# Key preparation only behind decay steps, two gate tiles ahead of the last merge, and a later transpose in z

## The chip, the cores and the metric

The kernel runs on one core of a Trainium2 chip. The metric is the device time of one execution in microseconds (us), from the first to the last instruction. The engines are named as in the profile: PE is TensorE's matmuls, PEld its weight loads, DVE VectorE, ACT ScalarE, POOL GpSimd and SP SyncE, whose queue issues the DMAs. Each engine works through its own queue in order and waits on semaphores for the others.

## The reference

Two layers of a hybrid mixer over 512 latent and 256 context tokens, in float32, with 1024 channels. Each layer normalises its input, makes one input projection and runs three branches over it: attention (8 query heads, 2 key heads, normalised queries and keys with rotary positions), a bidirectional state-space scan (SSD) in chunks of 128 tokens, and a gated convolution of 31 taps. The branches are merged by sigmoid gates and projected back. Cut to what matters here:

```python
q, k, v, ga, xbc, dt, z, glu, gcv, gm = split_in(h @ w_in)
qh = apply_axial_rope(rmsnorm(heads_q(q), q_norm_w), rope)
kh = apply_axial_rope(rmsnorm(heads_kv(k), k_norm_w), rope)
ua = merge_heads(latent_attention(qh, kh, heads_kv(v), kh_c, vh_c)) * jax.nn.silu(ga)
us = rmsnorm(y * jax.nn.silu(z), ssd_norm_w)          # y: the scan's output
uc = conformer_conv(glu, gcv, cm_conv_w, cm_conv_b, cm_ln_w, cm_ln_b)
g = jax.nn.sigmoid(gm.reshape(gm.shape[:-1] + (N_BRANCH, D_MODEL)) + b_gate)
y = (g[..., 0, :] * (ua @ w_br_attn) + g[..., 1, :] * (us @ w_br_ssd)
     + g[..., 2, :] * (uc @ w_br_conv))
x_new = x + gate * (y @ w_out)
```

In the last layer context tokens give only keys, values and scan states, so most tiles there have 512 columns in place of 768.

## The kernel before, in words

Every product of a float32 activation with a weight is made of three matmuls: both operands are split into a rounded high part and a remainder (`hh` and `hl`, `whi` and `wlo`). `wload` loads a weight tile (`raw`) and splits it on ScalarE (`whi`, L156) and VectorE (`wlo`, L157). Channel-major products run through `mm_cm_steps` (L175), 24 matmuls for 8 input tiles or 12 for 4, with two accumulator banks (`pj`).

A layer goes through these stages: the convolution branch's projection; keys, values and step sizes (`ps_kvd`); the eight x, B and C tiles (`ps_xbc`); z (`ps_z`); queries (`ps_q`); layer norm of the convolution; the scan with the merge of the convolution branch as filler; attention with the merge of the scan branch as filler; the merge of the attention branch; the output projection (`ps_o`). From the key projection to the end of attention the order of TensorE's instructions is as the code is written; the other engines' order, and TensorE's outside that stretch, is set by a scheduler.

Three things are touched by the change.

*The B tiles.* Tiles 0 to 5 of x and B are transposed (`xbc_turn`, `pt_x`) some tiles after their projection: the loop over `ps_xbc` takes them from the list `late` once it holds two, which leaves the last (tile 5, the second B tile) for the loop over z. The first B tile is transposed in the loop over `ps_xbc`.

*Key preparation.* `qk_prep` makes a key pair (`khl`, into `kk`) or a query pair (`qhl`, into `qt`) of 256 tokens ready in three turns: first squares (`qsq`), their sum (`qrs`, with a power on GpSimd) and the rotation, then the split into high part and remainder, then eight transposes (`pt_qk`), which ScalarE empties bank by bank. `Pipe.turn` moves each pair in work on by one turn and starts the next: three key pairs, then query pairs. The list `main` holds the steps of the scan: `begin`, `decay` (matrices `am` and `al`, matmuls `pseg`, `ew`, `wt`), `inner` (matmuls `pyd` on `wt`), `state` and `end`. After each step `sf.fill` issues some matmuls of the filler (merge `ps_gm` and `ps_br`, attention gates `ps_ga`, gate tiles made ahead). Once the filler's merge is done, every other step is followed by a turn. After the `us` transposes the rest of the turns follow, until three key pairs and one query pair are done:

```python
while pipe.done < NTT // 2 + 1:
    sf.fill(qk_turns / 2)
    pipe.turn()
```

with `qk_turns` 2 in the first layer and 0 in the second. Then attention begins with `ps_l`, the scores, which feed `mx` and the exponentials (`pe`).

*The last merge.* `merge_steps` goes over eight channel tiles. For each it makes the gate (`sig_steps`: 24 matmuls `ps_gm`, then `tg` on ScalarE), or loads it if it was made ahead (`AHEAD_TILES`, the odd ones), multiplies the branch output (`ps_br`) by it, adds the sum so far (`yo`, loaded) and splits the result (`yh`, `yl`). `tg`, `yo` and the loaded attention outputs (`og`) share three buffers (`fill`). Just before, attention ends with `po_v`, `oa` and the split `ua`.

Of the kernel before, what the change touches and what calls it, by code (L numbers as in the profile page):

```python
# [15 lines left out]
P = 128  # L16
DM = 1024
KD = DM // P
# [39 lines left out]
def hybrid_kernel(ctx, tc, xT, cc, consts, rope, mod_params, params, fnw, w_mod, w_cm, w_q, w_kvd, w_z,  # L58
# [18 lines left out]
    def bigt(shape, dt, name):  # L77
        return big.tile(shape, dt, tag="S", name=name)

    def work(shape, dt, name):  # L80
        return wk.tile(shape, dt, tag="W", name=name)

    def small(shape, dt, name):
        return wk.tile(shape, dt, tag="W2", name=name, bufs=7)

    def fill(shape, name):
        return fl.tile(shape, F32, tag="F", name=name)
# [52 lines left out]
    def wload(src, nk, ncol, prio=TOP, keep=None):  # L140

        per, half = {P: (8, 4), 256: (4, 2)}.get(ncol, (2, 2))
        res = []
        with tc.high_priority(offset=prio):
            for k0 in range(0, nk, per):
                n = min(per, nk - k0)
                raw = wp.tile([P, n, ncol], F32, tag="raw", name="raw")
                nc.sync.dma_start(raw, src[:, k0:k0 + n, :])
                for u0 in range(0, n, half):
                    m = min(half, n - u0)  # L150
                    if keep is None:
                        hi = wp.tile([P, m, ncol], F32R, tag="whi", name="whi", bufs=5)
                        lo = wp.tile([P, m, ncol], F32R, tag="wlo", name="wlo", bufs=5)
                    else:
                        hi, lo = (keep[:, i, k0 + u0:k0 + u0 + m, :] for i in range(2))
                    S.activation(hi, raw[:, u0:u0 + m, :], AF.Copy)  # L156
                    V.tensor_tensor(out=lo, in0=raw[:, u0:u0 + m, :], in1=f(hi), op=ALU.subtract)  # L157
                    res += [(hi[:, i, :], lo[:, i, :]) for i in range(m)]
        return res

    def mm_cm_steps(w, xh, xl, ntok, evac, name, col=slice(None), psum=None, late=False, piece=PIECE):

        nk = len(w)
        spans = ntok if isinstance(ntok, tuple) else [(a, min(ntok, a + 512)) for a in range(0, ntok, 512)]
        for a, b in spans:
            ps = (psum or pjt)(name)
            done = 0  # L170
            order = [(k, w[k][i], x) for k in range(nk) for i, x in ((0, xh), (0, xl), (1, xh))]
            if late:
                order.sort(key=lambda o: o[2] is xl)
            for n, (k, st, mv) in enumerate(order):
                T.matmul(ps[:, :b - a], st[:, col], mv(k)[:, a:b], start=(n == 0), stop=(n == len(order) - 1))  # L175
                done += b - a
                if done >= piece and n < len(order) - 1:
                    yield done
                    done = 0
            evac(ps[:, :b - a], a, b)  # L180
            yield done
# [28 lines left out]
    def mm_tm(w, xh, xl, tt, ncol, name):  # L210
        ps = pjt(name)
        nk = len(w)
        t = tok(tt)
        for k in range(nk):
            hi, lo = w[k]
            T.matmul(ps[:, :ncol], xh(k)[:, t], hi, start=(k == 0), stop=False)
            T.matmul(ps[:, :ncol], xh(k)[:, t], lo, start=False, stop=False)
            T.matmul(ps[:, :ncol], xl(k)[:, t], hi, start=False, stop=(k == nk - 1))
        return ps
# [153 lines left out]
    for li in range(2):  # L373
        last = li == 1
        par = sm.tile([P, NPAR], F32, tag="par", name="par")
        nc.sync.dma_start(par, params[li])
        ntok = NL if last else NT
# [73 lines left out]
        def conv(n, after=None):  # L451
            with tc.issue_after(after.ins) if after is not None else nullcontext():
                for _ in range(n):
                    next(taps, None)

        for ct in range(4):
# [10 lines left out]
            tg = fill([P, ntok], "tgl")  # L467
# [72 lines left out]
        late, soon = [], []  # L540
# [42 lines left out]
        for b in range(2):  # L583
            w = wload(w_z[li, b], KD, 256)
            for tt in range(ntt):
                ps = mm_tm(w, xh, xl, tt, 256, "ps_z")
                zs = small([P, 256], F32, "zs")
                S.activation(zs, ps[:, 0:256], AF.Silu)
                for fn in soon:
                    fn()  # L590
                soon = []
                nc.sync.dma_start(z_dr[tt][:, b * 256:(b + 1) * 256], zs)
                if late and tt > 0:
                    late.pop(0)()
                conv(2, xm)

# [86 lines left out]
        def then(fn, steps):  # L683

            done = 0
            for n in steps:
                yield n
                done += n
                if done >= MOD_LAG and fn is not None:
                    fn()  # L690
                    fn = None
            if fn is not None:
                fn()

        def sig_steps(br, ct, tg):
            w = wload(w_cm[li, C_GM + br * 8 + ct], KD, P)
            yield from mm_cm_steps(w, xh, xl, ntok,
                                   lambda ps, a, b: S.activation(tg[:, a:b], ps, AF.Tanh, scale=0.5,  # L698
                                                                 bias=hw[:, br * 8 + ct:br * 8 + ct + 1]), "ps_gm")
# [8 lines left out]
        def merge_steps(br, u, first, fin, ready=()):  # L708
            if fin:
                yh.extend(bigt([P, 4, ntok], F32R, "yh") for _ in range(2))  # L710
                yb = bigt([P, 4, ntok], F32R, "yl")
                yl.extend([yb[:, i, :] for i in range(4)] + [work([P, ntok], F32R, "yl") for _ in range(4)])
            end = None
            next_mods = Mods(1, mods[1], 8 * (2, 1, 0)[br])
            for ct in range(KD):
                if ct % 2 == 0:
                    wb = wload(w_br[li, br, ct // 2], 4, 256)
                if not first:
                    yo = fill([P, ntok], "yo")
                    nc.sync.dma_start(yo, y_dr[ct][:, :ntok])  # L720
                if ct in ready and not last:
                    tg = mid.tile([P, ntok], F32, tag="H", name="tgr", bufs=2)
                else:
                    tg = fill([P, ntok], "tg")
                c0 = (ct % 2) * P

                def br_out(ps, a, b):
                    V.scalar_tensor_tensor(out=tg[:, a:b], in0=tg[:, a:b], scalar=1.0, in1=ps, op0=ALU.add,  # L728
                                           op1=ALU.mult)

                if ct in ready:
                    nc.sync.dma_start(tg, g_dr[ct][:, :ntok])
                else:
                    yield from then(end, sig_steps(br, ct, tg))
                    end = None
                yield from then(end, mm_cm_steps(wb, lambda k: u[0][:, k, :], lambda k: u[1][:, k, :], ntok, br_out,
                                                 "ps_br", slice(c0, c0 + P)))
                end = None
                if not first:
                    V.tensor_tensor(out=tg, in0=tg, in1=yo, op=ALU.add)  # L740
                if not fin:
                    nc.sync.dma_start(y_dr[ct][:, :ntok], tg)
                else:
                    a, b = yh[ct // 4][:, ct % 4, :], yl[ct]
                    S.activation(a, tg, AF.Copy, scale=0.5)
                    V.scalar_tensor_tensor(out=b, in0=tg, scalar=0.5, in1=f(a), op0=ALU.mult, op1=ALU.subtract)
                if not last and ct % 2 == 1:
                    end = next_mods.visit()
                    yield 2048
            if end is not None:  # L750
                end()
# [204 lines left out]
        decays = [partial(ch.decay, g) for ch in chunks for g in range(2)]  # L956
# [28 lines left out]
                   len(main) + end_turns + 4 * us_turns + qk_turns)  # L985
        pipe, kk = Pipe(), None

        since = 0
        for step in main:
            step()  # L990
            sf.fill()
            if merged[0]:
                if kk is None:
                    kk = bigt([P, 2, KVH, NT], F32R, "kk")
                    qts.append(bigt([P, 4, ntok], F32R, "qt"))
                    pipe.todo += [partial(k_prep, t0) for t0 in range(0, NTT, 2)]
                    pipe.todo += [partial(q_prep, 0, t0) for t0 in range(0, ntt, 2)]
                since += 1
                if since % 2 == 1:
                    pipe.turn()  # L1000
        sf.fill(end_turns)

# [1 line left out]
        for ct in range(4):  # L1004
            nw = par[:, O_SNW + ct:O_SNW + ct + 1]
            for t0, t1 in ((0, NLT), (NLT, ntt))[:1 if last else 2]:
# [3 lines left out]
                a, b, n = t0 * P, t1 * P, (t1 - t0) * P  # L1010
# [318 lines left out]
```

## Time and profile before

| what | us |
|---|---|
| times shown, lowest, median, highest | 1477.03, 2856.81, 3255.66 |
| the profiled execution, own time | 1479.32 |
| its span, first to last instruction | 1477.5 |
| PE busy | 1434.7 |
| PEld busy | 1256.6 |
| DVE busy | 1037.4 |
| ACT busy | 712.7 |

The profile is of one execution. Busy times of different engines overlap. The ends of matmuls are modelled, so the starts tell more than the durations. The granted clock is given as a share of TensorE's full 2.4 GHz: 1.00, or 0.50 for 1.2 GHz.

### The profile page before, as it was taken

Reading aid. Unit: us, or ns where it says so; the run is one execution under the profiler, and the core shown is the slowest. Engines: PE = TensorE matmul, PEld = TensorE weight load, DVE = VectorE, ACT = ScalarE, POOL = GpSimd, SP = SyncE. Lnnn points to the kernel's source line nnn. Section 1 sums busy time; section 2 is a strip of 40 time slices with the busy share of each in tenths; the row PEclk is TensorE's granted clock in tenths of the full one; section 3 lists DMA queues with packets and bytes.
Section 4 is the critical chain, followed back from the end, with each engine's and each line's share of the span. In section 5 each row is a group of like instructions: output and inputs, shape, how many; then the busy total and the mean of one; then the engine's idle time right before and its main releaser. Section 6 shows DMA issues by size and latency. Waiting matters only on the chain. (4 is left out here: it accounts for less than half of the span.)

```text
span 1477.5 us, 24830 instructions
## 1 busy us (share of the span) xinstructions
PE 1434.7 (97%) x9660; PEld 1256.6 (85%) x9660; DVE 1037.4 (70%) x1895; ACT 712.7 (48%) x1580; POOL 81.0 (5%) x177
## 2 busy tenths in 40 slices
PE   5999999999998999999999999999999999999996
PEld 5889899988887888888888888989988887888796
DVE  5689998766557766565444478899877788676464
ACT  4423543365444466566322344354464646666341
POOL 0000010100001210000000000001010121000000
PEclk9999999999999999999999999999999999999998
DMA  9222333213334323323654433223423342323451
GB/s 375 76 73 95 103 126 111 77 61 100 101 105 126 132 90 120 101 74 120 201 170 156 162 118 113 69 62 115 141 76 114 97 145 93 100 93 105 146 171 58
DMA packets 79670, 172.57 MB, mean 117 GB/s; under 512 B 7616, under 2 KB 37440, under 8 KB 79552
## 3 DMA queue, kind: packets, MB, share of 16 engines
q1 hardware_dynamic: 79552, 170.98, 35.3%
q8 instruction: 76, 1.25, 0.4%
q14 instruction: 42, 0.34, 0.1%
HBM read 143.43 MB, written 27.53 MB: 116 GB/s over the span
## 5 line engine op out<-in xcount | busy, mean ns | idle before, releaser
L156 ACT ACTIVATE whi<-raw 128x512 fp32r<-128x512 f32 (+1 forms) x316 | 198.9, 632 | 269.3 <-DMA raw<-in_w_cm_dram 57.1
L157 DVE TENSOR_TENSOR wlo<-raw,whi 128x512 fp32r<-128x512 f32 (+1 forms) x316 | 217.2, 692 | 149.0 <-ACT whi L156 138.2
L445 DVE SCALAR_TENSOR_TENSOR vacc<-vt,par,vacc 128x783 f32<-128x783 f32 (+1 forms) x232 | 206.3, 889 | 8.9 <-ACT vacc L442 5.4
L175 PE MATMUL ps_gm<-hh,whi 128*128 128x512 f32 (+1 forms) x576 | 210.4, 365 | 0.0
L175 PE MATMUL ps_gm<-hh,wlo 128*128 128x512 f32 (+1 forms) x576 | 207.5, 360 | 0.0
L175 PE MATMUL ps_gm<-hl,whi 128*128 128x512 f32 (+1 forms) x576 | 207.4, 360 | 0.0
L175 PEld LDWEIGHTS ps_gm<-hh,whi 128*128 128x128 f32 x576 | 109.1, 189 | 16.5 <-issue 1.5
L175 PEld LDWEIGHTS ps_gm<-hh,wlo 128*128 128x128 f32 x576 | 108.9, 189 | 16.1 <-issue 0.7
L175 PEld LDWEIGHTS ps_gm<-hl,whi 128*128 128x128 f32 x576 | 108.9, 189 | 15.0 <-issue 0.5
L175 PE MATMUL ps_xbc<-hh,whi 128*128 128x512 f32 (+1 forms) x240 | 83.5, 348 | 0.0
L175 PE MATMUL ps_xbc<-hl,whi 128*128 128x512 f32 (+1 forms) x240 | 82.4, 343 | 0.0
L175 PE MATMUL ps_xbc<-hh,wlo 128*128 128x512 f32 (+1 forms) x240 | 82.3, 343 | 0.0
L698 ACT ACTIVATE tg<-ps_gm,hw 128x512 f32<-128x512 f32 x72 | 44.5, 617 | 46.3 <-PE ps_gm L175 45.2
L175 PE MATMUL ps_o<-yh,whi 128*128 128x256 f32 (+1 forms) x208 | 65.8, 317 | 0.5 <-DVE xnew L1158 0.3
L175 PE MATMUL ps_o<-yh,wlo 128*128 128x256 f32 (+1 forms) x208 | 65.8, 316 | 0.0
L175 PE MATMUL ps_o<-yl,whi 128*128 128x256 f32 (+1 forms) x208 | 65.7, 316 | 0.0
L1078 ACT ACTIVATE pth<-pt_p 128x512 f32<-128x512 f32 x72 | 43.3, 604 | 46.0 <-PE pt_p L1072 45.3
L567 DVE SCALAR_TENSOR_TENSOR xacc<-xraw,par,xacc 128x770 f32<-128x770 f32 (+1 forms) x64 | 63.2, 997 | 1.9 <-ACT xacc L564 1.6
L728 DVE SCALAR_TENSOR_TENSOR tg<-tg,ps_br 128x512 f32<-128x512 f32 x66 | 39.6, 600 | 32.6 <-PE ps_br L175 28.8
L1034 DVE TENSOR_REDUCE mx<-ps_l 128x1 f32<-128x512 f32 x64 | 43.5, 688 | 22.7 <-PE ps_l L1028 22.3
L175 PE MATMUL ps_br<-us,whi 128*128 128x512 f32 (+1 forms) x192 | 57.0, 364 | 0.0
L175 PE MATMUL ps_br<-ua,whi 128*128 128x512 f32 (+1 forms) x192 | 54.3, 368 | 2.6 <-ACT ua L1142 2.2
(281 smaller groups left out, 3619.0 us busy)
## 6 DMA issues: line engine op xcount, KB each, us to landing
raw<-in_w_cm_dram SPq DMA_DIRECT2D x96, 512.0 KB, 3.5
raw<-in_w_mod_dram SPq DMA_DIRECT2D x32, 512.0 KB, 5.3
raw<-in_w_br_dram SPq DMA_DIRECT2D x24, 512.0 KB, 3.7
raw<-in_w_out_dram SPq DMA_DIRECT2D x21, 512.0 KB, 3.7
wm<-in_w_mod_dram SPq DMA_DIRECT2D x16, 512.0 KB, 8.9
ydr<-tg SPq DMA_DIRECT2D x16, 384.0 KB, 3.2
yo<-ydr SPq DMA_DIRECT2D x16, 384.0 KB, 3.3
raw<-in_w_z_dram SPq DMA_DIRECT2D x8, 512.0 KB, 3.7
```

Source lines behind the costliest of these rows:

```text
L156: S.activation(hi, raw[:, u0:u0 + m, :], AF.Copy)
L157: V.tensor_tensor(out=lo, in0=raw[:, u0:u0 + m, :], in1=f(hi), op=ALU.subtract)
L175: T.matmul(ps[:, :b - a], st[:, col], mv(k)[:, a:b], start=(n == 0), stop=(n == len(order) - 1))
L445: V.scalar_tensor_tensor(out=acc[:, :n] if j else vt[:, o:o + n], in0=vt[:, o + j:o + j + n], scalar=cw(j), in1=acc[:, :n], op0=ALU.mult, ...
L567: xm = V.scalar_tensor_tensor(out=acc[:, :n], in0=raw[:, j:j + n], scalar=par[:, O_SCW + ct * 5 + j:O_SCW + ct * 5 + j + 1], in1=acc[:, :n ...
L698: lambda ps, a, b: S.activation(tg[:, a:b], ps, AF.Tanh, scale=0.5, bias=hw[:, br * 8 + ct:br * 8 + ct + 1]), "ps_gm")
L728: V.scalar_tensor_tensor(out=tg[:, a:b], in0=tg[:, a:b], scalar=1.0, in1=ps, op0=ALU.add, op1=ALU.mult)
L1034: V.tensor_reduce(out=mx[:, 0, j:j + 1], in_=pl[j], axis=AX.X, op=ALU.max, negate=True)
L1078: S.activation(pf, pt, AF.Copy)
```

## The change

A turn of the key preparation follows only a decay step in place of every other step. In the last merge of the second layer two gate tiles that were not made ahead (channel tiles 0 and 2) are made before the first `ps_br`, and their later place in the loop is skipped. The last B tile's transposes move from the second token tile of z's first half to the first token tile of its second half.

```diff
-                if late and tt > 0:
+                if late and b == 1:
                     late.pop(0)()
...
+            early = {}
+            if fin and last:
+                for ct in [ct for ct in range(KD) if ct not in ready][:2]:
+                    early[ct] = fill([P, ntok], "tg")
+                    yield from sig_steps(br, ct, early[ct])
+            done = set(early)
             for ct in range(KD):
...
-                if ct in ready and not last:
+                if ct in early:
+                    tg = early.pop(ct)
+                elif ct in ready and not last:
                     tg = mid.tile([P, ntok], F32, tag="H", name="tgr", bufs=2)
...
                 if ct in ready:
                     nc.sync.dma_start(tg, g_dr[ct][:, :ntok])
-                else:
+                elif ct not in done:
                     yield from then(end, sig_steps(br, ct, tg))
                     end = None
...
-        since = 0
         for step in main:
             step()
             sf.fill()
...
-                since += 1
-                if since % 2 == 1:
+                if step in decays:
                     pipe.turn()
```

What it does to the queues shows at three places.

ScalarE in the first layer, at the last decay step of the scan; before:

```order
L817 ACTIVATE wt<-gm_4506,dts 128x128 x4
L861 ACTIVATE qsq<-ks 128x256
L665 ACTIVATE ga<-ps_ga 128x512
L156 ACTIVATE whi<-raw 128x512
L889 ACTIVATE khl<-ks 128x2x64 x4
L805 ACTIVATE am<-cst,dah 128x128 x4
L156 ACTIVATE whi<-raw 128x512
L805 ACTIVATE am<-cst,dah 128x128
L665 ACTIVATE ga<-ps_ga 128x256
L805 ACTIVATE am<-cst,dah 128x128 x3
```

And with the change:

```order
L825 ACTIVATE wt<-gm_4506,dts 128x128 x4
L813 ACTIVATE am<-cst,dah 128x128 x8
L869 ACTIVATE qsq<-ks 128x256
L665 ACTIVATE ga<-ps_ga 128x512
L156 ACTIVATE whi<-raw 128x512 x2
L665 ACTIVATE ga<-ps_ga 128x256
L821 ACTIVATE ew<-pseg 128x512
L825 ACTIVATE wt<-gm_4506,dts 128x128 x4
L897 ACTIVATE khl<-ks 128x2x64 x8
```

The eight `am` of the last decay step now stand directly behind `wt`, ahead of the keys' `qsq` and `khl`; both key pairs' `khl` stand behind the next `wt`.

TensorE and ScalarE in the second layer, ahead of the first scores; TensorE before:

```order
L1009 MATMUL pt_us<-mr,xt 128x128 x4
L175 MATMUL ps_gm<-hh,whi 128x512
L175 MATMUL ps_gm<-hl,whi 128x512
L175 MATMUL ps_gm<-hh,wlo 128x512
L175 MATMUL ps_gm<-hh,whi 128x512
L175 MATMUL ps_gm<-hl,whi 128x512
L175 MATMUL ps_gm<-hh,wlo 128x512
L903 MATMUL pt_qk<-mr,khl 128x128 x16
L903 MATMUL pt_qk<-mr,qhl 128x128 x8
L1028 MATMUL ps_l<-kk,qt 128x512 x2
```

TensorE with the change:

```order
L175 MATMUL ps_gm<-hh,whi 128x512
L175 MATMUL ps_gm<-hl,whi 128x512
L175 MATMUL ps_gm<-hh,wlo 128x512
L911 MATMUL pt_qk<-mr,khl 128x128 x24
L911 MATMUL pt_qk<-mr,qhl 128x128 x8
L1034 MATMUL ps_l<-kk,qt 128x512 x2
```

ScalarE there, before:

```order
L861 ACTIVATE qsq<-qs 128x512
L1011 ACTIVATE us<-pt_us,par 128x512
L156 ACTIVATE whi<-raw 128x512
L698 ACTIVATE tg<-ps_gm,hw 128x512
L904 ACTIVATE kk<-pt_qk 128x4x128 x4
L904 ACTIVATE qt<-pt_qk 128x4x128 x2
L896 ACTIVATE qhl<-qs 128x4x64 x2
L1050 ACTIVATE pe,sr<-ps_l,mx 128x512
```

And with the change:

```order
L897 ACTIVATE khl<-ks 128x2x64 x8
L1017 ACTIVATE us<-pt_us,par 128x512
L156 ACTIVATE whi<-raw 128x512
L698 ACTIVATE tg<-ps_gm,hw 128x512
L912 ACTIVATE kk<-pt_qk 128x4x128 x2
L869 ACTIVATE qsq<-qs 128x512
L912 ACTIVATE kk<-pt_qk 128x4x128 x4
L904 ACTIVATE qhl<-qs 128x4x64 x2
L912 ACTIVATE qt<-pt_qk 128x4x128
```

All three key pairs and the first query pair are now transposed in one row. The `qsq` that stood in this stretch was the second query pair's; now it is the first's, which has yet to be rotated, split and transposed before `ps_l`. In the first layer the same stretch has 24 transposes in a row, where it had eight.

ScalarE at the end of attention in the second layer, where the gate tiles `tg` meet the split `ua`; before:

```order
L698 ACTIVATE tg<-ps_gm,hw 128x512
L156 ACTIVATE whi<-raw 128x512
L1142 ACTIVATE ua<-oa 128x512
L1142 ACTIVATE ua<-og 128x512 x2
L698 ACTIVATE tg<-ps_gm,hw 128x512
L1142 ACTIVATE ua<-og 128x512
L156 ACTIVATE whi<-raw 128x512 x2
L745 ACTIVATE yh<-tg 128x512
```

And with the change:

```order
L156 ACTIVATE whi<-raw 128x512
L698 ACTIVATE tg<-ps_gm,hw 128x512
L1148 ACTIVATE ua<-oa 128x512
L1148 ACTIVATE ua<-og 128x512 x2
L698 ACTIVATE tg<-ps_gm,hw 128x512
L156 ACTIVATE whi<-raw 128x512
L1148 ACTIVATE ua<-og 128x512
L156 ACTIVATE whi<-raw 128x512
L698 ACTIVATE tg<-ps_gm,hw 128x512
```

A third `tg` comes ahead of the first `yh`. On TensorE 28 `ps_gm` matmuls follow the last `po_v` where six did, and 48 `ps_br` in a row follow them where 24 did.

## Rows read from the trace of the kernel before

**Rows 1.** The page, part 1: busy us, share of the span, instructions.
```profile
PE 1434.7 (97%) x9660; PEld 1256.6 (85%) x9660; DVE 1037.4 (70%) x1895; ACT 712.7 (48%) x1580; POOL 81.0 (5%) x177
```

**Rows 2.** Waits of PE, whole span: total us, times, longest us.
```profile
PE pseg L810 <- ACT am L805: 3.7, 3, 2.0
...
PE ps_br L175 <- ACT ua L1142: 2.2, 1, 2.2
```

**Rows 3.** Windows: length, busy us (instructions) by engine, granted clock, DMA share, GB/s.
```profile
463.00:466.40 3.40, 1.30 (x4) 0.78 (x5) 3.40 (x13) 3.09 (x10) 0.00 (x0) 1.00 0.60 178
466.40:469.90 3.50, 3.50 (x10) 2.71 (x9) 2.74 (x10) 2.16 (x7) 1.21 (x2) 0.51 0.65 184
...
1224.20:1227.60 3.40, 3.40 (x11) 2.63 (x10) 2.55 (x5) 0.72 (x2) 0.00 (x0) 0.50 0.00 0
...
1377.80:1381.20 3.40, 3.40 (x9) 2.48 (x8) 0.69 (x1) 1.44 (x3) 0.00 (x0) 0.50 0.45 147
```

**Rows 4.** Timeline, first layer, last decay step: start us, us, instruction, idle before.
```profile
463.88 0.50 PE L810 MATMUL pseg<-am,mr 128*128 128x512 f32 x1 [2.04 <-ACT am L805]
...
465.83 0.50 PE L810 MATMUL pseg<-am,mr 128*128 128x512 f32 x1 [1.22 <-ACT am L805]
...
468.56 0.43 DVE L867 TENSOR_TENSOR ks<-ks,qrs 128x256 f32<-128x256 f32 x1 [0.39 <-POOL qrs L138]
...
470.17 0.68 DVE L820 TENSOR_TENSOR wt<-wt,ew 128x512 f32<-128x512 f32 x1
...
470.75 1.00 PE L831 MATMUL pyd<-xt,wt 128*128 128x64 f32 x8
...
472.12 1.39 DVE L769 TENSOR_TENSOR xd<-xt,dd 128x512 f32<-128x512 f32 x1
```

**Rows 5.** Timeline, second layer, round the first scores.
```profile
1201.70 0.80 PE L903 MATMUL pt_qk<-mr,khl 128*128 128x128 f32 x8
...
1202.33 1.96 PE L846 MATMUL po<-st,bc 128*128 128x256 f32 x8
...
1218.31 0.63 ACT L861 ACTIVATE qsq<-qs 128x512 f32<-128x512 f32 x1 [0.89 <-DMA qs<-qdr]
...
1218.97 0.69 DVE L865 TENSOR_REDUCE qrs<-qsq 128x8 f32<-128x512 f32 x1 [0.77 <-ACT qsq L861]
...
1219.76 1.14 PE L903 MATMUL pt_qk<-mr,khl 128*128 128x128 f32 x12
...
1220.88 2.05 ACT L904 ACTIVATE kk<-pt_qk 128x512 fp32r<-128x512 f32 x4
...
1222.02 1.02 PE L903 MATMUL pt_qk<-mr,qhl 128*128 128x128 f32 x8
...
1223.47 0.73 PE L1028 MATMUL ps_l<-kk,qt 128*128 128x512 f32 x2 [0.44 <-ACT qt L904]
...
1225.31 0.75 DVE L897 TENSOR_TENSOR qhl<-qs,qhl 128x256 fp32r<-128x256 f32 x2
```

**Rows 6.** Timeline, second layer, end of attention.
```profile
1373.54 0.67 ACT L698 ACTIVATE tg<-ps_gm,hw 128x512 f32<-128x512 f32 x1
...
1375.82 0.49 PE L175 MATMUL ps_br<-ua,whi 128*128 128x512 f32 x1 [2.15 <-ACT ua L1142]
1376.71 0.50 PE L175 MATMUL ps_br<-ua,whi 128*128 128x512 f32 x1 [0.40 <-DVE ua L1143]
```

**Rows 7.** The chain that ended last: start us, us, what.
```profile
1383.94 5.51 PE ps_gm L175 x24
1389.45 5.61 PE ps_br L175 x24
```

**Rows 8.** DMA issues from 1360 us on: KB each, median us to landing.
```profile
tg<-gdr SPq DMA_DIRECT2D x4, 256.0 KB, 2.6
```

**Rows 9.** Timeline, second layer, the two B tiles' transposes.
```profile
998.87 1.54 PE L537 MATMUL pt_x<-mr,bc 128*128 128x128 f32 x6 [2.40 <-ACT bc L573]
...
1012.43 0.82 PE L537 MATMUL pt_x<-mr,bc 128*128 128x128 f32 x6
```

## The prediction

> **What bounds the kernel now.** I read the page first, then the waits of TensorE, then the granted clock in windows round the waits, and last the timelines at the places that the change touches. The page has TensorE's matmuls busy for 97% of the span [rows 1]. The waits view gives the other side: behind the first weights, the waits that the change can reach are 3.7 us in three for the decay matrices (`pseg` on ScalarE's `am`) and 2.2 us for the attention output (`ps_br` on `ua`) [rows 2]. So VectorE and ScalarE set the time only where TensorE stands still, and an edit is worth what it takes from such a wait or adds to one. A wait has a second price: after three of them the granted clock is 0.51 or 0.50, the lower level, 1.2 GHz, for about 3.4 us, and ahead of the first of them TensorE had worked 1.30 us of 3.4 [rows 3]. At half clock 3.4 us do the work of 1.7, so such a stretch costs up to 1.7 us where TensorE is what the rest waits for.
>
> The sum is made against the profiled execution, 1479.32 us (span 1477.5 and 1.8 around it). That is the scale of the lowest shown time, 1477.03. The median, 2856.81, is nearly twice that; nothing in this trace accounts for it, so I forecast an execution like the profiled one.
>
> **Key preparation, layer 0, at the decay steps.** Before, ScalarE's order has `khl` between `wt` and `am`; `khl` needs VectorE's rotation of the keys, `am` stands behind it, and `pseg` starts at 463.88 after 2.04 us of waiting, then waits 1.2 us more [rows 2, 4]. The order of the changed kernel has all eight `am` ahead of `qsq` and `khl`, so these 3.3 us go. But what is late next? `pyd` needs `wt` times `ew`, which VectorE starts at 470.17 and ends at 470.85; `pyd` starts at 470.75 [rows 4]. VectorE is busy 3.40 us of 3.40 in 463.0 to 466.4 [rows 3]: it is the bound of this place. Ahead of that product its new order leaves out the third key tile's reduction, two multiplications (0.43 us for the one shown) and a `khl` pair (about as long), some 1.7 us as an estimate (four of 0.4), and puts in `xd`, which took 1.39 us before [rows 4]. So `pyd` comes 0.3 to 1.5 us earlier, not 3.3. TensorE then stands in front of `pyd` instead of `pseg`, over 3 us as an estimate (the 3.3 us and the part of the half-clock stretch that now runs full), and a half-clock stretch follows `pyd`, where TensorE is the bound; before, that stretch lay at 466.4 to 469.9 [rows 3], inside time in which `pyd` had to wait anyway. I take **0 us**, between -1.5 and +1.7.
>
> **Key preparation, layer 0, ahead of the first scores.** Two decay steps are left after the merge, so two turns happen there instead of five, and four remain for the loop after the decay chunks. There the matmuls that serve as filler run out: 24 `pt_qk` transposes stand in a row in front of `ps_l`, where eight stood before and the other eights lay among gate matmuls. In layer 1 the trace shows what 24 in a row cost: from 1219.76 to `ps_l` at 1223.47, 3.71 us, because ScalarE must empty a bank for every four (`kk` x4 in 2.05 us) [rows 5]. An eight among other work takes 0.63 us from its start to the next instruction (1201.70 to 1202.33) [rows 5]; three of them are 1.9. The difference is 1.8 us, and the layer 1 stretch was followed by 3.4 us at half clock [rows 3], up to 1.7 us more. I take **+3.5 us**, between +1.8 (no clock loss) and +4.1 (a `qsq` of 0.63 us now stands among the evictions).
>
> **Key preparation, layer 1.** Here no decay step follows the merge, so no turn happens in the main loop at all: all six follow the `us` transposes, without filler (its share is 0 turns in this layer), and 32 transposes stand in front of `ps_l`. Follow the first query pair, which is the last thing needed. TensorE reaches the transposes at 1219.76 less the eight that moved down, 1219.1 [rows 5]. ScalarE's new order is `whi`, `tg`, two `kk`, and only then the query's `qsq`. Before, the first `kk` starts 1.12 us after the transposes (1220.88) for the same `whi` and `tg` [rows 5]; so the two `kk` run from 1220.2 to 1221.3 and `qsq`, 0.63 us, ends at 1221.9 [rows 5]. From the reduction of a pair to the end of its `qhl` VectorE, GpSimd and ScalarE took 7.1 us (1218.97 to 1225.31 + 0.75) [rows 5], the next pair's preparation, which is the same code. That gives 1229.0; its first half is done 0.3 us earlier. From the query's transposes to `ps_l` it was 1.45 us (1222.02 to 1223.47) [rows 5]. So `ps_l` starts near 1230.1 instead of 1223.47: +6.7 us. Behind it the next pair's `qhl` stands in ScalarE's queue after the four exponentials of the first unit, which I put at +1 us, with the clock. I take **+7.7 us**. Bounds: +5.5, if `kk` need not wait for `whi` and `tg` (1.1 us less), and +10, if the next pair is late by as much as a clock stretch more.
>
> **The two gate tiles ahead of the last merge.** Before, six gate matmuls follow the last `po_v`, and `ps_br` waits 2.15 us for `ua`, then 0.40, with a half-clock stretch behind (1.7 us) [rows 2, 3, 6]: at most 4.3 us can come back. After, 28 follow. But the second gate tile needs the accumulator bank of the tile before, and ScalarE's order empties that behind `oa` and a `whi`: in the trace this `tg` starts at 1373.54 and ends at 1374.21 [rows 6]. TensorE runs dry some 0.6 us before, at 1375.82 - 2.15 = 1373.67 [rows 6], since four of the 28 don't need that bank and two more now stand ahead of `po_v`. From 1374.3, 24 matmuls at 5.51 us and 24 `ps_br` at 5.61 [rows 7] end at 1385.4. Before, the same work ended at 1383.94 + 5.51 = 1389.45 [rows 7]. That is 4.0 us gained. Of this some is given back: four products now follow one another, and the fourth needs the bank of the second, whose gate tile is loaded into one of three buffers only when the first product is done with it; the loads here take 2.6 us (median) to land [rows 8]. Product one ends at 1382.7, its five steps on VectorE and ScalarE free the buffer about 2.6 us later, the load lands near 1387.9 and is used up by 1389.5, where the fourth product could start at 1388.2: 1.3 us. I take **-2.8 us**, between -4.3 and -1.
>
> **The last B tile's transposes in the second half of z.** These start at 1012.43 in layer 1 without a wait; the 2.40 us wait stands at 998.87, at the B tile before, which the loop over x, B and C transposes itself and which the condition changed here does not touch [rows 9]. Moving transposes that did not wait costs and gives **0**; their eviction moves with them, and its reader comes long after. If it made `zs` late, it would be by one `bt` eviction, under 1 us.
>
> **The sum.** 0 + 3.5 + 7.7 - 2.8 + 0 = +8.4 us: 1479.3 + 8.4 = **1488 us**, 0.6% slower. All ends together give +1.5 to +14.8, 1481 to 1494.
>
> **Rivals.** *TensorE has slack.* If stalls on it were made up elsewhere, as an engine off the critical path would, the time stays at 1479. For it speaks the weight-load share of 85% [rows 1]; against it that the last chain runs from matmul to matmul without a pause [rows 7]. Chance 0.10. The Trainium skill, "Perfetto Trace Analysis", section Identifying the Most-Contended Engine, says that matmul busy time is no good measure of headroom and weight-load busy time is; by it 15% of the span would be free, and this rival would be the forecast, while by the chain rows it is not.
>
> *The waits go and the keys come in time* (the other side: faster). If VectorE finished the query pair of layer 1 by the time TensorE arrives, as 1223.5 did before, the layer costs 0 instead of 7.7, and the decay waits give their 3.3 us: 1479.3 - 3.3 - 4.3 + 1.8 = 1473.5. It decides from the point at which `qsq` of the query stands ahead of the `kk`; the order says it doesn't. Chance 0.07.
>
> *Late queries through all of attention* (clearly slower). Each of the eight later query pairs would reach its scores late by the 2.5 us of layer 0's evictions plus a clock stretch: 8 x 4.2 = 34 us, 1522 with the forecast's 8. It needs VectorE to stay behind; once the first scores run, the preparation before was ready in time. It decides if a pair's 7.1 us exceed what a unit leaves. Chance 0.03.
>
> **How the numbers follow.** The forecast has 0.78, the three rivals 0.20, and 0.02 is for what I don't see. The range reaches down past the absorbed case, to 1476, and up to 1496, two us over the bounds for what a count by hand misses: it leaves out the faster and the clearly slower rival. A change of 2% (30 us) is about what a measurement of this kernel can tell from none; all but the last rival lie within it: faster 0.01, same 0.95, slower 0.04.
>
> **What would show it.** Right: in layer 1 `ps_l` waits some 7 us for `qt` and the waits view has `pt_qk` on `qhl` high; in layer 0 `pseg` no longer waits, `pyd` waits instead, and 24 transposes end in a wait of 1 to 2 us; `ps_br` no longer waits for `ua`, but a short wait stands between the third and fourth product; the 2.40 us at the other B tile are unchanged. Wrong: `ps_l` of layer 1 within 3 us of the transposes, or `pyd` of layer 0 on time.

## The result, and the profile after

The changed kernel takes 1499.79 us (median of four runs, 1497.03 to 1500.7): 1.0127 times the kernel before, with a 95% interval of 1.0113 to 1.0142. On the scale of the profiled execution of before that is 1.27% of 1479, some 19 us slower, where 8.4 us were forecast and 1496 was the upper end. Two of the four times of before beside it (2856.81 and 3255.66) are of disturbed executions and left out of the ratio.

The page of the changed kernel, part 1, as [rows 1]:

```profile
PE 1438.5 (96%) x9660; PEld 1259.0 (84%) x9660; DVE 1039.9 (69%) x1895; ACT 712.1 (48%) x1580; POOL 77.4 (5%) x177
```

TensorE does the same number of instructions in 3.8 us more busy time; the span grew by 20.7 us, to 1498.2. So most of the time went into waits. The waits of TensorE in the changed kernel (total us, times, longest us), as [rows 2]:

```profile
PE pt_qk L911 <- DVE qhl L905: 7.5, 3, 5.9
PE po_v L1097 <- ACT pth L1084: 3.6, 2, 2.8
PE ps_l L1034 <- ACT pe L1056: 3.6, 2, 2.0
...
PE ps_br L175 <- DVE tg L736: 2.1, 2, 1.3
...
PE ps_ga L175 <- DVE ga L666: 1.7, 1, 1.7
...
PE ps_gm L175 <- ACT tg L698: 1.1, 1, 1.1
PE pseg L818 <- ACT am L813: 0.4, 1, 0.4
```

The old waits are gone or small (`pseg` on `am` from 3.7 to 0.4, `ps_br` on `ua` from 2.2 to none). In their place stand `pt_qk` on `qhl`, which the forecast named, and two that it did not price: the scores `ps_l` on the exponentials `pe`, and `po_v` on `pth`, 3.6 us each.

To place the time, the table takes the starts of the same matmuls in two traces: how much each stretch of the program grew against the kernel before (us). The stretches end at the first `ps_ga` of the first layer (450.67 in before, 454.44 in after), its first `pt_us` (506.02, 504.02), first `ps_l` (522.16, 524.27) and last `ps_l` (690.10, 702.97), then at the last `pt_us` of the second layer (1218.26, 1231.01), its first `ps_l` (1223.47, 1243.77), last `ps_l` (1355.09, 1376.70) and first `ps_o` (1417.09, 1437.87). The lower lines are the experiments below.

| kernel | start to `ps_ga` | decay steps | to first scores | attention, layer 0 | to layer 1's `pt_us` | to first scores | attention, layer 1 | last merge |
|---|---|---|---|---|---|---|---|---|
| changed | +3.8 | -5.8 | +4.1 | +10.8 | -0.1 | +7.5 | +1.3 | -0.8 |
| e2_gates | +3.3 | +0.6 | 0.0 | +0.1 | -0.1 | 0.0 | 0.0 | -1.1 |
| e3_l1_old | +2.9 | -5.8 | +4.3 | +10.7 | +0.2 | 0.0 | -0.1 | -1.3 |
| e4_split_later | -0.9 | -4.0 | +4.1 | +2.1 | -1.6 | +7.5 | +0.2 | -1.6 |
| e5_spread | +5.3 | -3.6 | 0.0 | 0.0 | -1.4 | 0.0 | -1.5 | -1.3 |
| e6_no_start | +2.0 | -5.7 | +4.8 | +2.6 | -0.6 | +7.6 | +1.5 | -1.4 |
| e7_no_split | +0.6 | -5.9 | +4.1 | +3.1 | -0.6 | +7.6 | +0.5 | -1.6 |
| e8_both | -0.6 | -3.8 | -0.2 | +2.1 | -0.9 | +0.3 | +0.3 | -1.5 |
| e9_z | 0.0 | -0.2 | 0.0 | 0.0 | +0.1 | 0.0 | 0.0 | 0.0 |
| e10_split_behind | +3.5 | -5.9 | +4.1 | +5.4 | -0.5 | +7.9 | +1.5 | -0.8 |
| e11_third | +3.6 | -3.7 | 0.0 | 0.0 | 0.0 | 0.0 | -1.5 | -3.5 |
| e12_spread_only | +1.9 | -3.8 | 0.0 | 0.0 | +0.2 | 0.0 | 0.0 | +0.2 |

The first column varies from run to run (-0.9 to +5.3, last section), with and without each part of the change, and is not explained by it. In the changed kernel 24 transposes moved from the decay steps to the stretch behind them; at the 0.63 us for eight of [rows 5] that is 1.9 us, so the decay steps gained 3.9 and the way to the first scores lost 2.2. The largest entry, +10.8, lies behind the first scores of the first layer.

*That entry.* The timelines there, first the kernel before, then the changed one (start us, us, instruction, idle before):

```profile
522.16 0.63 PE L1028 MATMUL ps_l<-kk,qt 128*128 128x512 f32 x2
...
526.07 0.69 ACT L1050 ACTIVATE pe<-ps_l,mx 128x512 f32<-128x512 f32 x1 [2.78 <-DVE mx L1041]
```

```profile
524.27 0.73 PE L1034 MATMUL ps_l<-kk,qt 128*128 128x512 f32 x2 [0.95 <-ACT qt L912]
...
534.63 0.73 PE L1034 MATMUL ps_l<-kk,qt 128*128 128x512 f32 x2 [1.53 <-ACT pe L1056]
...
546.66 0.73 PE L1034 MATMUL ps_l<-kk,qt 128*128 128x512 f32 x2 [2.02 <-ACT pe L1056]
...
556.36 0.91 PE L1097 MATMUL po_v<-pth,vv 128*64 128x128 f32 x6 [2.79 <-ACT pth L1084]
...
530.08 0.73 ACT L904 ACTIVATE qhl<-qs 128x256 fp32r<-128x256 f32 x2 [5.37 <-DVE qs L886]
531.60 0.69 ACT L698 ACTIVATE tg<-ps_gm,hw 128x512 f32<-128x512 f32 x1 [0.79 <-ACT qhl L904]
532.79 0.60 ACT L912 ACTIVATE qt<-pt_qk 128x512 fp32r<-128x512 f32 x1 [0.51 <-PE pt_qk L911]
533.29 0.62 ACT L869 ACTIVATE qsq<-qs 128x512 f32<-128x512 f32 x1
533.80 0.68 ACT L1056 ACTIVATE pe<-ps_l,mx 128x512 f32<-128x512 f32 x1
...
529.24 0.15 DVE L1047 TENSOR_TENSOR mx<-mx 128x2 f32<-128x2 f32 x1
```

Before, the exponentials start 3.9 us after the scores, as soon as `mx` is there. After, they start 9.5 us after them: ScalarE's queue has the second query pair's `qhl`, a gate tile, that pair's `qt` and the third pair's `qsq` ahead of them, and `qhl` waits 5.4 us for a rotation that VectorE has only now come to. `mx` itself was ready at 529.4. The next scores then wait for their bank until the exponentials have emptied it. The exponentials of the next two units are as late: 11.2 and 10.7 us behind their scores (534.63 to 545.83, 546.66 to 557.38), and 5.4 at the fourth. At the second unit ScalarE waits ahead of them for gate matmuls (2.0 us) and a loaded weight tile (1.3 us), not for a `qhl`; at the third a `qhl` again waits 5.4 us for a rotation.

The waits of TensorE in this stretch are 6.8 us (3.6 for `pe`, 2.8 for `pth`, 0.4 for `pt_p`), against 0.3 before. Behind them the granted clock falls to 0.50, 1.2 GHz, twice (windows of the changed kernel, in the order of columns of [rows 3]):

```profile
535.80:539.20 3.40, 3.40 (x15) 3.21 (x15) 2.80 (x7) 2.18 (x5) 0.83 (x1) 0.50 0.00 0
556.30:559.70 3.40, 3.34 (x32) 3.35 (x34) 1.52 (x4) 2.86 (x11) 0.72 (x2) 0.50 0.01 2
```

At half clock each does the work of 1.7 us. So 6.5 of the 10.8 us are waits, and about 3.4, an estimate, the clock; before has no such stretch in this layer's attention.

*The decay steps* (TensorE of the changed kernel):

```profile
466.60 0.50 PE L175 MATMUL ps_ga<-hh,whi 128*128 128x512 f32 x1 [1.66 <-DVE ga L666]
...
467.17 0.40 PE L818 MATMUL pseg<-am,mr 128*128 128x512 f32 x1
...
470.85 0.89 PE L839 MATMUL pyd<-xt,wt 128*128 128x64 f32 x7
...
472.00 0.69 DVE L828 TENSOR_TENSOR wt<-wt,ew 128x512 f32<-128x512 f32 x1
```

`pseg` no longer waits, and `pyd` does not wait either: it starts 1.15 us ahead of the product `wt` times `ew` that the forecast had it wait for. It reads the `wt` of two decay steps earlier (`ahead` is 2 in the code).

*The second layer's first scores:*

```profile
1232.51 1.14 PE L911 MATMUL pt_qk<-mr,khl 128*128 128x128 f32 x12
...
1242.36 1.23 PE L911 MATMUL pt_qk<-mr,qhl 128*128 128x128 f32 x8 [5.87 <-DVE qhl L905]
1243.77 1.22 PE L1034 MATMUL ps_l<-kk,qt 128*128 128x512 f32 x2 [0.18 <-ACT qt L912]
...
1234.77 0.64 ACT L869 ACTIVATE qsq<-qs 128x512 f32<-128x512 f32 x1
...
1241.34 0.72 ACT L904 ACTIVATE qhl<-qs 128x256 fp32r<-128x256 f32 x2 [3.98 <-DVE qs L886]
...
1250.39 0.69 ACT L1056 ACTIVATE pe<-ps_l,mx 128x512 f32<-128x512 f32 x1 [0.84 <-DVE mx L1047]
```

From the first transposes to `ps_l` it is 11.3 us, against the 11.0 of the forecast (1219.1 to 1230.1). Here the exponentials stand ahead of the next `qhl` and wait for `mx` alone.

*The last merge:*

```profile
1396.23 0.50 PE L175 MATMUL ps_gm<-hh,whi 128*128 128x512 f32 x1 [1.06 <-ACT tg L698]
1411.14 0.73 PE L175 MATMUL ps_br<-ua,whi 128*128 128x512 f32 x2 [0.78 <-DVE tg L736]
1421.12 0.74 PE L175 MATMUL ps_br<-ua,whi 128*128 128x512 f32 x2 [1.34 <-DVE tg L736]
...
1410.39 0.69 DVE L736 SCALAR_TENSOR_TENSOR tg<-tg,ps_br 128x512 f32<-128x512 f32 x1 [1.69 <-PE ps_br L175]
1412.48 0.69 DVE L736 SCALAR_TENSOR_TENSOR tg<-tg,ps_br 128x512 f32<-128x512 f32 x1 [1.40 <-DMA tg<-gdr]
...
1420.37 0.69 DVE L736 SCALAR_TENSOR_TENSOR tg<-tg,ps_br 128x512 f32<-128x512 f32 x1 [1.02 <-DMA tg<-gdr]
```

The wait for `ua` is gone; one for the bank (1.06 us) and two for VectorE's `tg` stand in its place. The second `ps_br` wait ends with a `tg` that waits for its load (1420.37). The first ends with the `tg` of 1410.39, which VectorE did ahead of one that waits for its load (1412.48). That late loads, and so the buffers, are behind both is not in these rows alone; e11 below shows it.

### The profile page after: what moved, and what is told of

It reads as the page before. It is cut to its first block, busy times and chain, and to the rows that moved or that the text cites. A ratio compares the mean times of both kernels' runs of the same rounds, so it can differ in the third digit from the quotient of the medians.

```text
span 1498.2 us, 24825 instructions
## 1 busy us (share of the span) xinstructions
PE 1438.5 (96%) x9660; PEld 1259.0 (84%) x9660; DVE 1039.9 (69%) x1895; ACT 712.1 (48%) x1580; POOL 77.4 (5%) x177
## 4 chain that ended last, share of the span: by engine, by line
PE 85%; DVE 6%; ACT 4%; DMA 3%; issue 2%; POOL 0%; SPq 0%; POOLq 0%; DVEq 0%; ACTq 0%
PE ps_gm L175 19%; PE ps_br L175 10%; PE ps_xbc L175 8%; PE ps_o L175 7%; PE ps_ga L175 4%; PE ps_u L175 4%; PE ps_g L175 4%; PE ps_gcv L175 3%; PE po_v L1097 3%; PE pt_p L1078 3%; PE ps_l L1034 2%; PE ps_q L217 1%; PE ps_q L216 1%; PE ps_q L218 1%; PE pseg L818 1%
## 5 line engine op out<-in xcount | busy, mean ns | idle before, releaser
L1097 PEld LDWEIGHTS po_v<-pth,vv 128*64 128x64 f32 x832 | 46.6, 140 | 11.2 <-issue 4.7
```

The lines of the kernel that those rows point to most:

```text
L1097: T.matmul(po[64 * j:64 * j + 64, tok(n)], vv[:, k0 + k, g, :], pths[k // 2][:, k % 2, j, :], start=(k == 0), stop=(k == nk - 1), tile_pos ...
```

## The experiments

Two theories for the 10.8 us. One: ScalarE's queue has the second pair's split ahead of the first unit's exponentials. The other: the pairs themselves are late, whatever the order. The rest of the runs take the parts one by one. Ratios are to the kernel before, with 95% intervals.

**e2_gates: the early gate tiles alone** (of the diff, only the hunks with `early` and `done`).

> The kernel before with the two early gate tiles alone. My forecast for this part was -2.8 us. The trace of the changed kernel suggests less: from the end of the last values (po_v) to the last matmul of the merge it is 1.2 us shorter than before, with a 1.1 us wait for the bank (tg) and two waits for VectorE's tg of 0.8 and 1.3 us. Theory A (those waits eat the gain): 1 to 1.5 us faster than before, ratio 0.999. Theory B (my sum): ratio 0.998. Theory C (the part does nothing): 1.000.

1.0001 (0.9986 to 1.0016). In the trace the last merge is 1.1 us shorter, the size of theory A; the time can't tell that from nothing (theory C). The forecast's -2.8 was too much.

**e3_l1_old: the changed kernel, second layer with the old rule.**

```diff
+                since += 1
-                if step in decays:
+                if since % 2 == 1 if last else step in decays:
```

> The changed kernel, but in the second layer the turns follow every other step again. Theory A (each layer carries its own loss, about 8 us each, as the positions of the same matmuls in the two traces say): 8 us below the changed kernel, ratio to before about 1.007. Theory B (the loss of the second layer comes from somewhere else, or is made up by other work): as the changed kernel, 1.013. If the first layer's decay steps gained nothing (my forecast's 0), this kernel would be slower than the changed one less 8 us by as much.

1.0054 (1.0032 to 1.0075). The columns of the second layer go to 0.0 and -0.1, so its loss of 8.9 us (7.5 + 1.3, rounded) is all the turns'. By time it is 1.0127 - 1.0054, 0.7%, some 11 us, with wide intervals. The first layer's columns stay.

**e4_split_later: the last turn before attention only finishes the first query pair.**

```diff
-            def turn(self, start=True):
-                for g in list(self.live):
+            def turn(self, start=True, only=False):
+                for g in self.live[:1] if only else list(self.live):
...
-                if start and self.todo:
+                if start and not only and self.todo:
...
-            pipe.turn()
+            pipe.turn(only=pipe.done == NTT // 2)
```

> The changed kernel, but the last turn before attention only finishes the first query pair; the second pair is split one unit later. Theory A (in the first layer the exponentials of the first unit stand behind the second pair's qhl in ScalarE's queue, 9.5 us after the scores): the exponentials start 4 us or more sooner and the first layer gets back 4 to 6 us, ratio to before 1.009 or less. Theory B (VectorE's rotation of the second pair is late whatever the queue's order is): no more than 1 us back, ratio 1.012 to 1.013. In the second layer no change within 1 us, since there the exponentials follow mx at once.

1.0037 (1.0024 to 1.0049), more than expected: attention of the first layer loses 2.1 us in place of 10.8. ScalarE now has the exponentials ahead of `qhl`:

```profile
521.47 1.22 PE L1034 MATMUL ps_l<-kk,qt 128*128 128x512 f32 x2 [0.95 <-ACT qt L912]
...
527.75 0.69 ACT L1056 ACTIVATE pe<-ps_l,mx 128x512 f32<-128x512 f32 x1 [5.85 <-DVE mx L1047]
...
529.99 0.73 ACT L904 ACTIVATE qhl<-qs 128x256 fp32r<-128x256 f32 x2
```

They start 6.3 us after the scores, when `mx` is there. Of the 2.1 us up to 1.7 are a half-clock stretch behind the first scores (0.50 from 521.0 to 524.4). But this kernel changes three things: the split, the start of the third pair, and the transposes' place on TensorE.

**e6_no_start and e7_no_split: one of the two delayed.** In e6 the last turn starts no pair but splits the second; in e7 it doesn't split the second but starts the third. First e6, then e7:

```diff
-            pipe.turn()
+            pipe.turn(start=pipe.done < NTT // 2)
```

```diff
-            def turn(self, start=True):
-                for g in list(self.live):
+            def turn(self, start=True, only=False):
+                for g in self.live[:1] if only else list(self.live):
...
-            pipe.turn()
+            pipe.turn(only=pipe.done == NTT // 2)
```

> The changed kernel, but the last turn before attention starts no further pair; it still finishes the first query pair and splits the second. Delaying split and start together gave back 0.9% (1.0037 against 1.0127). Theory A (what holds up the exponentials is the second pair's split, whose qhl stands ahead of them in ScalarE's queue): little comes back here, ratio to before 1.010 or more. Theory B (it is the third pair's start, with its loads, squares and rotation): nearly all comes back, ratio 1.006 or less.

> The changed kernel, but the last turn before attention finishes the first query pair and starts the third, without splitting the second. Theory A (the second pair's split in ScalarE's queue holds up the exponentials): nearly all of the 0.9% comes back, ratio to before 1.006 or less. Theory B (the third pair's start does it): little comes back, 1.010 or more. If both this kernel and the one without a start lie in between, the two share the loss.

1.0067 (1.0043 to 1.0091) and 1.0055 (1.0035 to 1.0074): e6 lies between its theories, nearer B; e7 lies in its theory A, though its interval reaches past it. Each takes most of the 10.8 us away (2.6 and 3.1 are left). As a way to tell split from start they failed, because the scheduler orders ScalarE anew in each: in e6, where the second pair is still split in that turn, its `qhl` falls behind the exponentials all the same.

```profile
528.43 0.69 ACT L1056 ACTIVATE pe<-ps_l,mx 128x512 f32<-128x512 f32 x1 [4.71 <-DVE mx L1047]
...
530.67 0.73 ACT L904 ACTIVATE qhl<-qs 128x256 fp32r<-128x256 f32 x2
```

So in e4, e6 and e7 alike the exponentials come first and the loss is mostly gone.

**e10_split_behind: only the split moves, behind the exponentials.** TensorE's order is that of the changed kernel, instruction by instruction; ScalarE's and VectorE's differ. (e7's edit, and behind the first unit's exponentials:)

```diff
         for _ in exps:
             wv.fill()
             wv.fill()
+        next(pipe.live[0])
```

> The changed kernel, with the same order of TensorE's instructions throughout; only the second pair's split is written behind the first unit's exponentials, so that ScalarE's order has the exponentials ahead of qhl, and VectorE's order follows. Theory A (the order of ScalarE's queue alone causes the loss behind the first scores of the first layer): the exponentials start 4 to 6.5 us after the scores in place of 9.5, and 7 to 10 us come back, ratio to before 1.004 to 1.008. Theory B (the loss is in the lateness of the second pair itself, or in its transposes' place on TensorE): the transposes still wait as before and no more than 2 us come back, ratio 1.011 or more.

1.0072 (1.0056 to 1.0088). That is in theory A's range; by the trace 5.4 us of the 10.8 come back and 5.4 are left, which is neither theory. The exponentials now wait for `mx` alone (7.1 us after the scores), and the other half shows on TensorE:

```profile
523.88 0.73 PE L1034 MATMUL ps_l<-kk,qt 128*128 128x512 f32 x2 [0.96 <-ACT qt L912]
...
534.80 0.52 PE L911 MATMUL pt_qk<-mr,qhl 128*128 128x128 f32 x4 [2.73 <-DVE qhl L905]
...
530.95 0.69 ACT L1056 ACTIVATE pe<-ps_l,mx 128x512 f32<-128x512 f32 x1 [4.03 <-DVE mx L1047]
...
533.76 1.35 ACT L904 ACTIVATE qhl<-qs 128x256 fp32r<-128x256 f32 x4
...
526.95 0.69 DVE L873 TENSOR_REDUCE qrs<-qsq 128x8 f32<-128x512 f32 x1 [0.63 <-ACT qsq L869]
...
530.16 0.69 DVE L875 TENSOR_TENSOR qs<-qs,qrs 128x512 f32<-128x512 f32 x1
530.76 0.15 DVE L1047 TENSOR_TENSOR mx<-mx 128x2 f32<-128x2 f32 x1
```

The second pair's transposes stand ahead of the second unit's scores and wait 2.7 us for a `qhl` that comes too late; a half-clock stretch (0.51 from 535.8 to 539.2) follows. Their place alone is not the reason. In e6 they stand at the same place, their `qhl` comes behind the exponentials too, and they wait 0.6 us:

```profile
531.70 0.50 PE L911 MATMUL pt_qk<-mr,qhl 128*128 128x128 f32 x4 [0.22 <-DVE qhl L905]
...
532.56 0.51 PE L911 MATMUL pt_qk<-mr,qhl 128*128 128x128 f32 x4 [0.36 <-DVE qhl L905]
```

What e6 leaves out in that turn is the start of the third pair. In e10 VectorE has that pair's reduction and first multiplication (526.95, 530.16) ahead of `mx`, so the exponentials start 7.1 us after the scores in place of 5.2 in e6, and the `qhl` behind them 9.9 in place of 7.4. So the order of ScalarE's queue, with VectorE's behind it, is worth half of the 10.8 us. Of the 5.4 left another 2.3 to 3.3 go where the third pair is started later (e6), the transposes come a unit later (e7, which still starts the third pair), or both (e4).

**e5_spread and e12_spread_only: turns on decay steps, then on every other step.** e5 has the other two parts of the change, e12 is the kernel before with this alone.

```diff
+            left -= step in decays
...
-                if step in decays:
+                if not left and step not in decays:
+                    since += 1
+                if step in decays or since % 2 == 1:
                     pipe.turn()
```

> The changed kernel with turns on decay steps while decay steps are left, and on every other step after the last of them. TensorE's order of key and query transposes is then as before in both layers, and only the first two turns of the first layer are moved off the steps between two decays. Theory A (the wait of pseg for am was worth its whole length, and the loss lies in the later turns alone): the first layer gains 4 to 5 us, the end 1, ratio to before 0.996. Theory B (my forecast: VectorE bounds pyd, so the first layer gains nothing): ratio 0.999 to 1.000.

> The kernel before with the spread turns alone, without early gates and with the transposes of the last B tile where they were. Theory A (what the spread turns gain is the wait of pseg for am at the last decay step of the first layer, about 3.6 us, with the half-clock stretch behind it): ratio 0.996 to 0.998. Theory B (the gain of 0.5% seen with all three parts came from the other two, or from their sum): ratio 0.999 to 1.000.

0.995 (0.9934 to 0.9967) and 0.9981 (0.9971 to 0.9991): both faster, theory A in both. The decay steps gain 3.6 and 3.8 us with no transposes moved, and the stretches to and through attention cost nothing. So the wait for `am` had a price, and the loss belongs to the turns that fell behind the scan. Part of the price is the clock: before has 0.50 from 466.4 to 469.8, these two and the changed kernel don't. e4, whose decay steps are the changed kernel's, has it from 463.0 to 466.4 and gains 4.0, less 1.9 for the transposes 2.1 us. Of e5's further gain 1.3 us is the last merge; -1.4 and -1.5 are half-clock stretches of before that this execution doesn't have (last section).

**e8_both: e5 with e4's later split.**

> The spread turns (ratio 0.995) together with the later split of the second pair: the candidate for the fastest. Theory A (the exponentials of the first unit are held up only where the turns are crowded): nothing more comes, ratio 0.994 to 0.996. Theory B (the split ahead of the exponentials costs something with spread turns too, since they started 3.9 us after the scores in the kernel before): 1 to 3 us more, ratio 0.993 to 0.994.

0.9982 (0.9968 to 0.9996): neither theory, slower than e5. Where the pairs are in time, splitting the second one unit later costs 2.1 us in the first layer's attention: a remedy for the crowded turns alone. Another 1.8 us against e5 lie in the second layer's attention, where e5 lacks a half-clock stretch that before and this run have.

**e9_z: the later transposes of the last B tile alone** (the first hunk of the diff).

> The kernel before with the later transposes of the last B tile alone. Theory A (they did not wait, so nothing changes): ratio 1.000 within 0.001. Theory B (the half-clock stretch behind the wait at the other B tile is shifted or given up): up to 1.5 us faster in each layer, ratio 0.998.

1.0006 (0.9995 to 1.0017), and no column off zero by more than 0.2: theory A, the forecast's 0.

**e11_third: e5, with the second early gate tile in another pool.**

```diff
-                    early[ct] = fill([P, ntok], "tg")
+                    early[ct] = mid.tile([P, ntok], F32, tag="H", name="tgr", bufs=2) if early else fill([P, ntok], "tg")
```

> The spread turns with the early gates, but the second early gate tile lies in another pool, so that the three shared buffers hold one tile less. Theory A (the two waits of ps_br for VectorE's tg, 0.8 and 1.3 us in the changed kernel, come from a loaded gate tile that has to wait for its buffer): both waits go or shrink below 0.5 us, and from the last values to the first output projection it is 1.5 to 2 us shorter than with early gates as they were. Theory B (they come from VectorE's own work or the accumulator banks): the waits stay. In the ratio to before 0.993 to 0.995 for A, 0.995 for B, hardly to be told apart by the time; the trace decides.

0.9935 (0.9918 to 0.9952), the fastest of all. The waits of TensorE from 1340 to 1465 us:

```profile
PE ps_rb L330 <- DVE dg L329: 2.2, 2, 1.4
PE ps_ss L318 <- DVE sq L305: 1.8, 1, 1.8
PE ps_gm L175 <- ACT tg L698: 1.1, 1, 1.1
...
```

No `ps_br` waits any more, and the last merge is 3.5 us shorter than before, 2.2 more than e5's: theory A, the buffers.

## Why the prediction was wrong

The forecast was slower, and it is slower, but by more than twice as much. By its own steps:

- **Layer 0 ahead of the first scores, forecast +3.5.** To the first `ps_l` the loss is 2.2 us net of the moved transposes, inside its bounds; the half-clock stretch that 1.7 of the 3.5 stood for does not follow there in the changed kernel. *The step that failed is its end:* I took the delay of the first scores for the whole price and priced nothing behind them in this layer, while 10.8 us lie there. For the second layer I had looked at where the next pair's `qhl` stands and found it behind the exponentials; in the first it stands ahead of them. The order of ScalarE that was there to read would have shown it. What the runs put in place of the step: half of the 10.8 us is ScalarE's order, with VectorE's behind it (e10), and some 8 us come back once the last turn starts no third pair (e6), leaves the second unsplit (e7), or both (e4).
- **Layer 0 at the decay steps, forecast 0 (-1.5 to +1.7).** Wrong, 3.6 to 3.9 us gained (changed kernel, e5, e12), 2.1 where the half-clock stretch stayed (e4). The wait of `pseg` was read rightly; what I put behind it was not. `pyd` at 470.75 [rows 4] has no idle time in its row: it followed its neighbours on TensorE. That a product ended at nearly the same time (470.85) I took for a cause, though `pyd` had started by then. The gain is below the 3.3 us of waits and the 1.7 of the half-clock stretch; `ps_ga` now waits 1.66 us for VectorE's `ga`.
- **Layer 1, forecast +7.7 (5.5 to 10).** Right: 8.9 us, of which 6.9 are the later first scores (7.5 less 0.6 for the eight transposes that moved), where the sum had 6.7, by the chain it named.
- **Early gate tiles, forecast -2.8 (-4.3 to -1).** The mechanism was right, its give-back mis-sized. With the buffers out of the way (e11) the merge gains 3.5, near the 4.0 of the first half of the step. I counted one late load of 1.3 us; there are two waits (0.78 and 1.34), and the bank cost 1.06 where I had 0.6. That left 0.8 to 1.6 us.
- **The last B tile, forecast 0.** Right (e9).

The five add up, in the profiled executions: -3.9 + 2.2 + 10.8 + 8.9 - 0.1 - 0.8 = 17.1 us, and with the 3.8 of the start 20.9, by rounding 0.1 more than the 20.8 by which the second layer's first `ps_o` is later (1417.09, 1437.87). The loss that I left out is 10.8 us; the gain that I left out, 3.9, took back part of it, so that the total came nearer to the forecast than its parts did.

Of the rivals, *late queries through all of attention* had the right mechanism in the wrong place: three units of the first layer, not eight pairs, after which the preparation catches up. I gave it 0.03 because I let it happen everywhere or nowhere. *The waits go and the keys come in time* had the decay steps right and layer 1 wrong. *TensorE has slack* is out: what its waits gained or lost (e3, e4, e12) came through to the end. So the row of PE at 97% decided, and not that of weight loads at 85%. The Trainium skill ("Perfetto Trace Analysis", Identifying the Most-Contended Engine) would have read the latter. The other page of the Trainium skill that bears on it is "PSUM — Partial Sum Buffer" (Engine vs sequencer instructions): the queues of ScalarE and VectorE are strictly first in, first out. The trace agrees: exponentials whose `mx` was ready at 529.4 waited until 533.8 behind a `qhl`.

What stays open: why the scheduler puts `qhl` ahead of the exponentials in the first layer of the changed kernel and behind them in the second was not tried. Nor was e10's order tried with VectorE's left as it was, so its half is that of both engines' new order.

## What to carry to other kernels

When preparation is moved nearer to its use, price the first user and then the next few: follow each in-order queue for some units beyond the first late result, and look at what the late work is now ahead of. Read a wait in the row of the one who waits; two times that nearly agree are no dependency. A tile made early holds its buffer and bank for longer, so count the whole ring, for every later user of it.

## What the runs showed that was not expected

*The start.* The first instruction that the change moves stands at 205.7 us in before, and yet the first `ps_kvd` (105.61 in before) came between 0.4 us sooner (e7) and 3.6 us later (e3). It lies in the first 37 us; between `ps_kvd` and the first `ps_ga` up to some 2 us more come in (e5). The same window of before and of the changed kernel (length, busy us and instructions by engine, granted clock, DMA share, GB/s):

```profile
25.60:34.00 8.40, 7.86 (x111) 6.54 (x111) 6.34 (x17) 4.16 (x8) 0.00 (x0) 1.00 1.02 408
```

```profile
25.60:34.00 8.40, 7.86 (x58) 6.12 (x55) 6.38 (x18) 4.16 (x8) 0.00 (x0) 1.00 1.03 409
```

In the same busy time TensorE gets through 58 matmuls of the sequence in place of 111. Half the matmuls in the same busy time is about what 1.2 GHz would give, and the trace of e12 does have 0.50 from 27.9 to 31.3 us. But the clock's row says 1.00 in both of these, so it does not show the cause. A single span against another is therefore good to about 5 us here; positions from a common instruction on do better.

*The half clock comes or stays away after the same wait.* `pt_x` waits 2.40 us for the first B tile in before [rows 9], in the changed kernel and in e5. The windows behind it, in this order:

```profile
998.90:1002.30 3.40, 3.40 (x11) 2.97 (x12) 3.40 (x6) 1.10 (x3) 0.00 (x0) 0.50 0.00 0
```

```profile
1012.10:1015.50 3.40, 3.40 (x18) 2.92 (x19) 3.40 (x6) 1.08 (x3) 0.00 (x0) 1.00 0.00 0
```

```profile
1000.80:1004.20 3.40, 3.40 (x18) 2.92 (x19) 3.40 (x6) 1.08 (x4) 0.00 (x0) 1.00 0.00 0
```

Only in before is it 1.2 GHz there, with 11 matmuls in place of 18; TensorE had done the same work and waited equally long in all three. So a half-clock stretch seen in one trace (here 7 of 18 matmuls, 1.3 of the 3.4 us) is no fixed price of its wait.
